# One decoder block on one core: weights stored in tiles, and two other ways to feed the gate and up products

## The chip, the cores and the metric

The kernel runs on 1 core of one Trainium2 chip. The time is device microseconds of one execution. Beside the timed runs there is one profiled execution, from which every duration below is taken. TensorE multiplies, VectorE (DVE in the profile) and ScalarE (ACT) work on tiles, SyncE (SP) issues the transfers, and PSUM is where TensorE's products land, in banks of 512 float32 columns.

## The reference

One decoder layer for 256 tokens of width 2048, all in float32:

```
h    = rmsnorm(x)
proj = h @ w_in                      # 2048 x 13328, for three branches and their gates
three branches (gated linear attention, stick-breaking attention,
cross-attention into 256 memory tokens), each projected to 2048
x    = x + (sum of sigmoid(gate) * branch) @ w_o
h2   = rmsnorm(x)
gate, up = split(h2 @ w_gate_up)     # 2048 x (5632 + 5632)
x    = x + (silu(gate) * up) @ w_down # 5632 x 2048
```

The change touches all large products by the layout of their weights, and the gate and up products of the last two lines by more than that.

## The kernel before, in words

**The large product.** Each large product goes through one function, `gemm`. It makes a block of 256 tokens x 512 columns as two PSUM tiles of 128 tokens (tag `acc`, four of them, so two blocks). To keep float32 accuracy, both sides are split into a high and a low part of few significant bits (`split`), in a type that TensorE multiplies in one pass (F32R), and three products are added: high times high, high times low, low times high. The activations (128 x 128 pieces of `hh` and `hl`, in other stages `xTh`/`xTl`, `oh`/`ol`, `fh`/`fl`) are the stationary operand, loaded by one LDWEIGHTS for each product (PEld in the profile); the weights (`whi`, `wlo`, 512 columns) are the moving operand, which is streamed past it.

**The staging.** A transfer on SyncE's queue brings 4 chunks of 128 weight rows x 512 columns (1 MB) into a tile `raw` (three buffers). The chunks are split in pairs: ScalarE copies a pair to `whi` (CAST, 128 x 1024), VectorE subtracts it from `raw` to give `wlo` (TENSOR_TENSOR, 128 x 1024). There are four buffers of each. A pair then feeds 12 products: for each of the two token tiles, for each of its two chunks, the three terms, on lines 169, 170 and 171.

**The order of the work.** The engines run their own instruction streams in the order in which a scheduler has put them; it goes by the order of the code and by when it expects operands and buffers. After each pair `step()` lets some small background work in, such as the transposes of a block of results (`to_chunks`, TensorE line 177).

**The feed-forward part.** For each of 11 blocks of 512 hidden columns: `gemm` for the gate (16 chunks, that is 8 pairs, 96 products), SiLU on ScalarE into `f_s` (line 717, two instructions), `gemm` for up (the same size), VectorE multiplies it into `f_s` (line 720), and `to_chunks` transposes and splits the block into `fh`/`fl` during the gate products that follow. After blocks 0 to 5 and 6 to 10 the down projection runs over what is there.

The lines of `before` that the prediction needs are 118 and 119 (the split), 158 (the load), 169 to 171 (the products), 177 (transposes), 475 to 477 (a small product for the low-rank columns with 256 moving columns), 357 (attention scores of plain float32), 717 and 720.

Of the kernel before, what the change touches and what calls it, by code (L numbers as in the profile page):

```python
# [10 lines left out]
F32R = mybir.dt.float32r  # L11
# [5 lines left out]
P = 128  # L17
# [12 lines left out]

O_GQ, O_GK, O_GV, O_GR, O_GA = 0, 512, 1024, 2048, 3072
O_SQ = O_GA + GR
O_SK, O_SV, O_MQ, O_G = O_SQ + MIX, O_SQ + 2 * MIX, O_SQ + 3 * MIX, O_SQ + 4 * MIX

# the gains, as columns of 128 rows
VECS = {
# [8 lines left out]
}  # L45
# constants that depend on shapes alone: for float32 operands, then for one-pass products
C_ID, C_STRICT, C_CAUSAL = 0, P, 2 * P
# [24 lines left out]
def trunk(ctx: ExitStack, tc: tile.TileContext, a, out):  # L72
# [18 lines left out]

    # ---- work that runs beside the large products: generators, advanced a step at a time
    background = []
# [12 lines left out]
    def pipelined(stages, n, gap):  # L106
        """One item enters per round; each of its stages comes gap rounds after the one before."""
        for r in range(n + gap * (len(stages) - 1)):
            for i in reversed(range(len(stages))):
                j = r - gap * i  # L110
                if 0 <= j < n:
                    stages[i](j)
                    yield

    def split(hi, lo, src, scale=None):
        """hi + lo = src (* scale), each part of 12 significant bits or fewer."""
        if scale is None:
            act.copy(hi, src)  # L118
            dve.tensor_tensor(lo, src, hi.bitcast(F32), op=ALU.subtract)  # L119
        else:  # L120
            act.activation(hi, src, AF.Copy, scale=scale)
            dve.scalar_tensor_tensor(lo, src, scale, hi.bitcast(F32), op0=ALU.mult, op1=ALU.subtract)

    def rsqrt_mean(ss, n, width):
        """(ss / n + eps) ** -0.5 of a [P, width] tile."""
        m = small.tile([P, width], F32, name="rs_m", bufs=4)
# [17 lines left out]

    def gemm(xs, w, c0, row0=0, first=()):
        """[T, NB] = xs.T @ w[row0*128.., c0:c0+NB] as two PSUM tiles of 128 tokens.
        xs: per chunk of 128 rows the high and low parts [P, T], or what loads them.
        first: the numbers of chunks in the first loads, where not KG."""
        o = [acc() for _ in range(2)]
        nk = len(xs)  # L150
        sizes = list(first)
        sizes += [min(KG, nk - k) for k in range(sum(sizes), nk, KG)]
        k0 = 0
        for n in sizes:
            xp = [x() if callable(x) else x for x in xs[k0 : k0 + n]]
            raw = loads()
            r0 = (row0 + k0) * P
            nc.sync.dma_start(raw[:, :n], w[r0 : r0 + n * P, c0 : c0 + NB].rearrange("(g p) n -> p g n", p=P))
            for g in range(0, n, 2):
                m = min(2, n - g)  # L160
                wh = wp.tile([P, 2, NB], F32R, tag="whi", name="whi")
                wl = wp.tile([P, 2, NB], F32R, tag="wlo", name="wlo")
                split(wh[:, :m], wl[:, :m], raw[:, g : g + m])
                for t in range(2):
                    s = slice(t * P, (t + 1) * P)
                    for j in range(m):
                        xh, xl = xp[g + j]
                        k = k0 + g + j
                        pe.matmul(o[t][:], xh[:, s], wh[:, j], start=k == 0, stop=False)  # L169
                        pe.matmul(o[t][:], xh[:, s], wl[:, j], start=False, stop=False)  # L170
                        pe.matmul(o[t][:], xl[:, s], wh[:, j], start=False, stop=k == nk - 1)  # L171
                step()
            k0 += n
        return o
# [4 lines left out]
    def load_T(pool_, name, src, gain, stage):  # L179
        """The transposed activations [D, T] times the gain, split, as chunks; the loads are traced  # L180
        where a chunk is first asked for."""
        hi = pool_.tile([P, KD, T], F32R, name=f"{name}h", tag=f"{name}h", bufs=1)
# [15 lines left out]
    def token_rstd(name, src, r, n):  # L198
        """(mean of squares of each row + eps) ** -0.5 into r [P, 2], its negative into n."""
        ss = const.tile([P, 2], F32, name=f"{name}_ss")  # L200
        for t in range(2):
            x = loads()[:].rearrange("p g n -> p (g n)")
            nc.sync.dma_start(x, src[t * P : (t + 1) * P, :])
            act.activation(x, x, AF.Square, accum_out=ss[:, t : t + 1])
            yield
        y = rsqrt_mean(ss[:], D, 2)
        dve.tensor_copy(r[:], y)
        dve.tensor_scalar(n[:], y, -1.0, None, op0=ALU.mult)

# [46 lines left out]

    # ---- the memory's keys and values
    w_in, w_kv = a["w_in"], a["w_mem_kv"]
# [44 lines left out]
    later, ones, tri, rest = (cr[:, i : i + P] for i in (R_LATER, R_ONES, R_TRI, R_REST))  # L303
    # q of the stick-breaking heads takes the factor d ** -0.5 with its gain
    g_sqs = const.tile([P, 1], F32, name="g_sqs")
# [40 lines left out]

    # ---- cross-attention into the memory
    o_mem = outT()
# [62 lines left out]

    # ---- stick-breaking attention
    o_sb = outT()
    W = 3 * P

    def diagonal(x):
        """Columns [0, 128) and [256, 384): the blocks on the diagonal."""
        return x[:, :W].rearrange("p (b q) -> p b q", b=3)[:, 0:3:2, :]
# [41 lines left out]

    # the low-rank columns as the stationary operand (with their neighbours): transposed at once
    a2 = att.tile([GR, 512], F32, name="a2", bufs=1)
# [3 lines left out]
    raw = wp.tile([P, KD, P], F32, tag="raw", name="raw_a", bufs=3)  # L466
    nc.sync.dma_start(raw[:], w_in[:, O_GA : O_GA + P].rearrange("(k p) n -> p k n", p=P))
    p = tmp()
# [13 lines left out]
    def sigmoid(dst, o, t, table):  # L482
        """Of the rows of o times their rstd; without the table, with the functions that the
        attentions hold loaded: exp(-log(1 + exp(-v)))."""
        if table:
# [9 lines left out]

    # ---- gated linear attention
    S = [att.tile([P, GDV], F32, name=f"S{h}", bufs=1) for h in range(GH)]
# [4 lines left out]
    def gla():  # L502
        for t in range(2):
# [57 lines left out]
            for c in range(2):  # L561
                s = slice(c * GC, (c + 1) * GC)
                for h in range(GH):
                    if c == 0:
                        # the first start clears what the bank has accumulated, for both of its heads
                        pe.matmul(ov[h], sT[:, h], vh[h], start=h % 2 == 0, stop=False, skip_group_check=True)  # L566
# [68 lines left out]

    # ---- merge of the branches
    merged = main.tile([P, 2, D], F32, name="merged", tag="resid")
# [19 lines left out]
    def turned_merged(n):  # L657
        i = n // NB
        if i % 2 == 0:
            # blocks 0 and 1 take the place of the stick-breaking heads', 2 and 3 that of the gates' inputs  # L660
            tm.append(
# [16 lines left out]

    # ---- output projection and residual
    hh = xpool.tile([P, KD, T], F32R, name="hh", tag="xTh")  # L680
# [22 lines left out]

    # ---- SwiGLU, the down projection in two parts of the hidden width
    ffn = ctx.enter_context(tc.tile_pool(name="ffn", bufs=1))
# [5 lines left out]
    for part in (range(0, 6), range(6, NF)):  # L711
        fs = []
        for j in part:
            g = gemm(hs, a["w_gate_up"], j * NB)
            sg = ffn.tile([P, 2, NB], F32, name="f_s", bufs=2)
            for t in range(2):
                act.activation(sg[:, t], g[t][:], AF.Silu, scale=r2[:, t : t + 1])
            u = gemm(hs, a["w_gate_up"], FF + j * NB)
            for t in range(2):
# [4 lines left out]
        for n in range(0, D, NB):  # L724
            o = gemm(fs, a["w_down"], n, row0=4 * part[0])
            for t in range(2):
                # the last piece in halves, so that its stores begin sooner
                half = NB // 2 if part[-1] == NF - 1 and n + NB == D else NB
# [37 lines left out]
```

## Time and profile before

| | |
|---|---|
| time, median of 2 runs | 1744.97 us (1744.42 to 1745.52) |
| span of the profiled execution | 1740.1 us |
| time less span | 4.9 us |
| TensorE busy, matrix products | 1728.5 us, 99%, 7588 records |
| TensorE busy, weight loads | 1387.5 us, 80% |
| VectorE busy | 924.7 us, 53% |
| ScalarE busy | 783.1 us, 45% |
| transfers | 321.8 MB, mean 185 GB/s |
| granted TensorE clock | 1.000 |

The profiled execution's own time is its span and the 4.9 us around it; its spans and the timed runs are compared on that footing. Rows of the time order have, from left to right, the start and the duration in us, the engine, the line of the kernel, the operation, output<-inputs, shapes, and how many records were merged. A product's duration of 0.39 to 0.40 us is modelled and overlaps the next one; what counts is the distance from one start to the next. In rows of groups the two numbers behind the bar are the busy time in us and the mean duration in ns, then the idle time before and what ended it.

### The profile page before, as it was taken

The numbers are of one execution on the slowest core, as the hardware profiler recorded it, in microseconds if no ns is written. First come the engines' busy times: TensorE is split into PE (matmuls) and PEld (weight loads), VectorE is DVE, ScalarE is ACT, GpSimd is POOL, SyncE is SP. The second block draws the span as 40 slices with busy tenths as digits, with TensorE's granted clock in tenths as the row PEclk, the third lists the DMA queues.
The fourth block names the chain that finished last, engine by engine and source line by source line (L and its number), as shares of the span: only waits on it lengthen the run. The fifth ranks groups of instructions, "written<-read, shape, count | busy, mean of one in ns | idle before, by whom it ended". The sixth has DMA issues, their size and how long they took to land.

```text
span 1740.1 us, 18823 instructions
## 1 busy us (share of the span) xinstructions
PE 1728.5 (99%) x7588; PEld 1387.5 (80%) x7588; DVE 924.7 (53%) x1082; ACT 783.1 (45%) x932; POOL 1.3 (0%) x6
## 2 busy tenths in 40 slices
PE   8999999999999999999999999999999999999999
PEld 6888888888777888888888888888888888888887
DVE  5756565664565555545555644444444444444543
ACT  6654444654554454344444444444433334444332
POOL 0000000000000000000000000000000000000000
PEclk9999999999999999999999999999999999999999
DMA  8775445445444565555556555555555555555553
GB/s 306 261 237 181 145 156 183 153 159 183 159 145 141 186 206 186 188 182 193 176 187 198 189 184 179 193 179 184 191 173 192 194 187 177 192 178 185 190 208 110
DMA packets 164310, 321.81 MB, mean 185 GB/s; under 512 B 5488, under 2 KB 12144, under 8 KB 163712
## 3 DMA queue, kind: packets, MB, share of 16 engines
q1 hardware_dynamic: 164048, 320.33, 54.7%
q8 instruction: 59, 0.97, 0.2%
q10 hardware_dynamic: 176, 0.30, 0.1%
q14 instruction: 27, 0.22, 0.0%
HBM read 318.50 MB, written 2.10 MB: 184 GB/s over the span
## 4 chain that ended last, share of the span: by engine, by line
PE 99%; DMA 1%; DVE 0%; ACT 0%; SPq 0%; issue 0%; DVEq 0%
PE acc L169 31%; PE acc L170 31%; PE acc L171 31%; PE tmp L177 2%; DMA raw<-in_w_mem_kv 1%; PE tmp L385 0%; PE tmp L357 0%; PE tmp L573 0%; PE tmp L568 0%; PE tmp L566 0%; PE tmp L442 0%; PE tmp L451 0%; PE tmp L425 0%; PE tmp L505 0%; PE tmp L475 0%; PE tmp L476 0%
## 5 line engine op out<-in xcount | busy, mean ns | idle before, releaser
L119 DVE TENSOR_TENSOR wlo<-raw,whi 128x1024 fp32r<-128x1024 f32 (+1 forms) x585 | 715.1, 1223 | 729.4 <-ACT whi L118 729.0
L118 ACT CAST whi<-raw 128x1024 fp32r<-128x1024 f32 (+1 forms) x585 | 611.4, 1046 | 870.2 <-PE acc L171 847.6
L169 PE MATMUL acc<-whi,xTh 128*128 128x512 f32 x832 | 335.4, 403 | 0.0
L171 PE MATMUL acc<-whi,xTl 128*128 128x512 f32 x832 | 329.1, 395 | 0.0
L170 PE MATMUL acc<-wlo,xTh 128*128 128x512 f32 x832 | 329.0, 395 | 0.0
L169 PE MATMUL acc<-whi,hh 128*128 128x512 f32 x704 | 279.9, 398 | 0.0
L171 PE MATMUL acc<-whi,hl 128*128 128x512 f32 x704 | 278.2, 395 | 0.0
L170 PE MATMUL acc<-wlo,hh 128*128 128x512 f32 x704 | 278.1, 395 | 0.0
L171 PEld LDWEIGHTS acc<-whi,xTl 128*128 128x128 f32 x832 | 156.0, 188 | 38.2 <-issue 0.3
L169 PEld LDWEIGHTS acc<-whi,xTh 128*128 128x128 f32 x832 | 156.2, 188 | 36.3 <-ACT whi L118 0.8
L170 PEld LDWEIGHTS acc<-wlo,xTh 128*128 128x128 f32 x832 | 156.3, 188 | 35.5 <-issue 0.7
L171 PEld LDWEIGHTS acc<-whi,hl 128*128 128x128 f32 x704 | 132.0, 188 | 32.2
L170 PEld LDWEIGHTS acc<-wlo,hh 128*128 128x128 f32 x704 | 132.1, 188 | 31.3
L169 PEld LDWEIGHTS acc<-whi,hh 128*128 128x128 f32 x704 | 132.1, 188 | 31.3
L169 PE MATMUL acc<-whi,fh 128*128 128x512 f32 x352 | 139.4, 396 | 0.0
L171 PE MATMUL acc<-whi,fl 128*128 128x512 f32 x352 | 139.1, 395 | 0.0
L170 PE MATMUL acc<-wlo,fh 128*128 128x512 f32 x352 | 139.1, 395 | 0.0
L169 PE MATMUL acc<-whi,oh 128*128 128x512 f32 x256 | 102.2, 399 | 0.0
L171 PE MATMUL acc<-whi,ol 128*128 128x512 f32 x256 | 101.3, 396 | 0.0
L170 PE MATMUL acc<-wlo,oh 128*128 128x512 f32 x256 | 101.2, 395 | 0.0
L171 PEld LDWEIGHTS acc<-whi,fl 128*128 128x128 f32 x352 | 66.0, 188 | 16.1
L169 PEld LDWEIGHTS acc<-whi,fh 128*128 128x128 f32 x352 | 66.0, 188 | 16.0
(205 smaller groups left out, 1191.1 us busy)
## 6 DMA issues: line engine op xcount, KB each, us to landing
raw<-in_w_in SPq DMA_DIRECT2D x104, 1024.0 KB, 5.0
raw<-in_w_gate_up SPq DMA_DIRECT2D x88, 1024.0 KB, 5.0
raw<-in_w_down SPq DMA_DIRECT2D x44, 1024.0 KB, 5.0
raw<-in_w_o SPq DMA_DIRECT2D x16, 1024.0 KB, 5.1
raw<-in_w_mem_kv SPq DMA_DIRECT2D x15, 1024.0 KB, 6.1
raw<-in_w_br_mem SPq DMA_DIRECT2D x8, 1024.0 KB, 5.0
raw<-in_w_br_sb SPq DMA_DIRECT2D x8, 1024.0 KB, 5.0
raw<-in_w_br_gla SPq DMA_DIRECT2D x8, 1024.0 KB, 5.0
```

Of the source, the lines that this page charges most:

```text
L118: act.copy(hi, src)
L119: dve.tensor_tensor(lo, src, hi.bitcast(F32), op=ALU.subtract)
L169: pe.matmul(o[t][:], xh[:, s], wh[:, j], start=k == 0, stop=False)
L170: pe.matmul(o[t][:], xh[:, s], wl[:, j], start=False, stop=False)
L171: pe.matmul(o[t][:], xl[:, s], wh[:, j], start=False, stop=k == nk - 1)
L177: pe.transpose(dst, src, ident)
```

## The change

It does three things.

1. **Tiled weights.** All large weights are laid out anew in memory before the launch, as [column block of 512][row within the chunk, 128][chunk][512 columns]. A load then reads, for each of the 128 partitions, one stretch of 4 x 2 KB where it read four stretches of 2 KB before. The 16 low-rank columns of `w_in` and their 112 neighbours become an array of their own (`w_ga`), read as 8 KB per partition, and the other columns of `w_in` move up by 16.
2. **Gate products, form "turns".** The 12 products of a pair change order: chunk, then term, then token tile. Each two neighbours have the same moving operand and write to the two PSUM tiles in turn.
3. **Up products, form "mixed".** High and low part of a pair share one tile `both` of 128 x 2 chunks x 512 columns x 2 parts; column n's high and low part lie next to each other. The CAST, the subtraction and the moving operand thus step over every other element (8 bytes from one to the next). `both` has two buffers, where `whi` and `wlo` have four each.

All other products keep the old form ("bank"). The core of the diff (removed comments left out):

```diff
-    def gemm(xs, w, c0, row0=0, first=()):
+    def gemm(xs, w, c0, row0=0, first=(), form="bank"):
...
-            r0 = (row0 + k0) * P
-            nc.sync.dma_start(raw[:, :n], w[r0 : r0 + n * P, c0 : c0 + NB].rearrange("(g p) n -> p g n", p=P))
+            r0 = row0 + k0
+            nc.sync.dma_start(raw[:, :n], w[c0 // NB, :, r0 : r0 + n])
             for g in range(0, n, 2):
                 m = min(2, n - g)
-                wh = wp.tile([P, 2, NB], F32R, tag="whi", name="whi")
-                wl = wp.tile([P, 2, NB], F32R, tag="wlo", name="wlo")
+                if form == "mixed":
+                    both = ffn.tile([P, 2, NB, 2], F32R, tag="both", name="both", bufs=2)
+                    wh, wl = both[:, :, :, 0], both[:, :, :, 1]
+                else:
+                    wh = wp.tile([P, 2, NB], F32R, tag="whi", name="whi")
+                    wl = wp.tile([P, 2, NB], F32R, tag="wlo", name="wlo")
                 split(wh[:, :m], wl[:, :m], raw[:, g : g + m])
-                for t in range(2):
-                    s = slice(t * P, (t + 1) * P)
-                    for j in range(m):
-                        xh, xl = xp[g + j]
-                        k = k0 + g + j
-                        pe.matmul(o[t][:], xh[:, s], wh[:, j], start=k == 0, stop=False)
-                        pe.matmul(o[t][:], xh[:, s], wl[:, j], start=False, stop=False)
-                        pe.matmul(o[t][:], xl[:, s], wh[:, j], start=False, stop=k == nk - 1)
+                def product(t, j, i):
+                    xh, xl = (x[:, t * P : (t + 1) * P] for x in xp[g + j])
+                    k = k0 + g + j
+                    pe.matmul(o[t][:], (xh, xh, xl)[i], (wh, wl, wh)[i][:, j],
+                              start=k == 0 and i == 0, stop=k == nk - 1 and i == 2)
+                if form == "turns":
+                    order = [(t, j, i) for j in range(m) for i in range(3) for t in range(2)]
+                else:
+                    order = [(t, j, i) for t in range(2) for j in range(m) for i in range(3)]
+                for q in order:
+                    product(*q)
...
-            g = gemm(hs, a["w_gate_up"], j * NB)
+            g = gemm(hs, a["w_gate_up"], j * NB, form="turns")
...
-            u = gemm(hs, a["w_gate_up"], FF + j * NB)
+            u = gemm(hs, a["w_gate_up"], FF + j * NB, form="mixed")
...
+    def tiled(w):
+        k, n = w.shape
+        return np.ascontiguousarray(w.reshape(k // P, P, n // NB, NB).transpose(2, 1, 0, 3))
```

**Where instructions move.** In the rows below, numbers tell buffers apart, and the shape is that of the output. First TensorE in the middle of a gate block; `acc` with the even and the odd number are the block's two token tiles. Before:

```order
L169 MATMUL acc_8035<-whi_8039,hh_6457 128x512
L170 MATMUL acc_8035<-wlo_8040,hh_6457 128x512
L171 MATMUL acc_8035<-whi_8039,hl_6458 128x512
L169 MATMUL acc_8035<-whi_8039,hh_6457 128x512
L170 MATMUL acc_8035<-wlo_8040,hh_6457 128x512
L171 MATMUL acc_8035<-whi_8039,hl_6458 128x512
L169 MATMUL acc_8036<-whi_8039,hh_6457 128x512
```

After the change, the same place in the pair `whi_7842`:

```order
L176 MATMUL acc_7722<-whi_7842,hh_6457 128x512
L176 MATMUL acc_7723<-whi_7842,hh_6457 128x512
L176 MATMUL acc_7722<-wlo_7843,hh_6457 128x512
L176 MATMUL acc_7723<-wlo_7843,hh_6457 128x512
L176 MATMUL acc_7722<-whi_7842,hl_6458 128x512
L176 MATMUL acc_7723<-whi_7842,hl_6458 128x512
```

Six products in a row went to one PSUM tile; now each goes to the other one than its predecessor. The number of products is the same.

Second, TensorE where an up block ends and the next gate block begins. Before, the last pair of up (`whi_8015`, into `acc_7894`) is followed by the first of the gate (`whi_8039`, into `acc_8035`):

```order
L169 MATMUL acc_7894<-whi_8015,hh_6457 128x512
L170 MATMUL acc_7894<-wlo_8016,hh_6457 128x512
L171 MATMUL acc_7894<-whi_8015,hl_6458 128x512
L169 MATMUL acc_8035<-whi_8039,hh_6457 128x512
L170 MATMUL acc_8035<-wlo_8040,hh_6457 128x512
```

After the change, at the last but one pair of up (`both_7977`, into `acc_7877` and `acc_7878`):

```order
L176 MATMUL acc_7878<-both_7960,hl_6458 128x512
L176 MATMUL acc_7877<-both_7977,hh_6457 128x512
L176 MATMUL acc_7878<-both_7977,hh_6457 128x512
L176 MATMUL acc_8011<-whi_8015,hh_6457 128x512
L176 MATMUL acc_8012<-whi_8015,hh_6457 128x512
L176 MATMUL acc_8011<-wlo_8016,hh_6457 128x512
L176 MATMUL acc_7877<-both_7977,hh_6457 128x512
L176 MATMUL acc_7877<-both_7977,hl_6458 128x512
```

Three products of the coming gate block (`acc_8011`, `acc_8012`) now stand between the high part of that pair and its low part.

Third, ScalarE from the SiLU of one block on. Before:

```order
L717 ACTIVATE f_s_7890<-acc_7739,r2_7107 128x512
L118 CAST whi_7947<-raw_7929 128x1024
L118 CAST whi_7965<-raw_7963 128x1024
L118 CAST whi_7981<-raw_7963 128x1024
L118 CAST whi_7999<-raw_7997 128x1024
L118 CAST whi_8015<-raw_7997 128x1024
L118 CAST whi_8039<-raw_8037 128x1024
```

After the change:

```order
L735 ACTIVATE f_s_7874<-acc_7723,r2_7107 128x512
L119 CAST both_7913<-raw_7911 128x1024
L119 CAST both_7928<-raw_7911 128x1024
L119 CAST both_7945<-raw_7943 128x1024
L119 CAST both_7960<-raw_7943 128x1024
L119 CAST whi_8015<-raw_8013 128x1024
L119 CAST whi_8038<-raw_8013 128x1024
L119 CAST both_7977<-raw_7975 128x1024
L119 CAST both_7992<-raw_7975 128x1024
```

The first two copies of the next gate block (`whi_8015`, `whi_8038`) now stand ahead of the last two of up (`both_7977`, `both_7992`); VectorE's subtractions follow the same order.

More of the change, by code (lines that the diff above doesn't have):

```diff
@@ L29 @@
 TAU = 16.0
-O_GQ, O_GK, O_GV, O_GR, O_GA = 0, 512, 1024, 2048, 3072
-O_SQ = O_GA + GR
+A_GA = 3072
+O_GQ, O_GK, O_GV, O_GR, O_SQ = 0, 512, 1024, 2048, 3072
 O_SK, O_SV, O_MQ, O_G = O_SQ + MIX, O_SQ + 2 * MIX, O_SQ + 3 * MIX, O_SQ + 4 * MIX
@@ L156, in gemm @@
             raw = loads()
-            r0 = (row0 + k0) * P
-            nc.sync.dma_start(raw[:, :n], w[r0 : r0 + n * P, c0 : c0 + NB].rearrange("(g p) n -> p g n", p=P))
+            r0 = row0 + k0
+            nc.sync.dma_start(raw[:, :n], w[c0 // NB, :, r0 : r0 + n])
             for g in range(0, n, 2):
                 m = min(2, n - g)
-                wh = wp.tile([P, 2, NB], F32R, tag="whi", name="whi")
-                wl = wp.tile([P, 2, NB], F32R, tag="wlo", name="wlo")
-                split(wh[:, :m], wl[:, :m], raw[:, g : g + m])
-                for t in range(2):
-                    s = slice(t * P, (t + 1) * P)
-                    for j in range(m):
-                        xh, xl = xp[g + j]
-                        k = k0 + g + j
-                        pe.matmul(o[t][:], xh[:, s], wh[:, j], start=k == 0, stop=False)
-                        pe.matmul(o[t][:], xh[:, s], wl[:, j], start=False, stop=False)
-                        pe.matmul(o[t][:], xl[:, s], wh[:, j], start=False, stop=k == nk - 1)
+                if form == "mixed":
[4 more added lines that the diff above has]
+                    wl = wp.tile([P, 2, NB], F32R, tag="wlo", name="wlo")
+                split(wh[:, :m], wl[:, :m], raw[:, g : g + m])
+                def product(t, j, i):
+                    xh, xl = (x[:, t * P : (t + 1) * P] for x in xp[g + j])
+                    k = k0 + g + j
+                    pe.matmul(
+                        o[t][:],
+                        (xh, xh, xl)[i],
+                        (wh, wl, wh)[i][:, j],
+                        start=k == 0 and i == 0,
+                        stop=k == nk - 1 and i == 2,
+                    )
+                if form == "turns":
[4 more added lines that the diff above has]
+                    product(*q)
                 step()
@@ L466, in trunk @@
     raw = wp.tile([P, KD, P], F32, tag="raw", name="raw_a", bufs=3)
-    nc.sync.dma_start(raw[:], w_in[:, O_GA : O_GA + P].rearrange("(k p) n -> p k n", p=P))
+    nc.sync.dma_start(raw[:], a["w_ga"])
     p = tmp()
@@ L751 @@
     }
+    def tiled(w):
+        k, n = w.shape
+        return np.ascontiguousarray(w.reshape(k // P, P, n // NB, NB).transpose(2, 1, 0, 3))
+    w = v["w_in"]
+    arrays["w_in"] = tiled(np.concatenate([w[:, :A_GA], w[:, A_GA + GR :]], 1))
+    arrays["w_ga"] = np.ascontiguousarray(w[:, A_GA : A_GA + P].reshape(KD, P, P).transpose(1, 0, 2))
+    arrays["gla_w_a2"] = v["gla_w_a2"]
     arrays["vecs"] = np.concatenate([cols(v[n]) for n in VECS], 1)
-    for n in ("w_in", "w_mem_kv", "gla_w_a2", "w_br_gla", "w_br_sb", "w_br_mem", "w_o", "w_gate_up", "w_down"):
-        arrays[n] = v[n]
+    for n in ("w_mem_kv", "w_br_gla", "w_br_sb", "w_br_mem", "w_o", "w_gate_up", "w_down"):
+        arrays[n] = tiled(v[n])
     nc = bacc.Bacc("TRN2", target_bir_lowering=False, num_devices=1)
```

## The prediction

> **What bounds the kernel now.** I read the page's engines and its chain of waits first, then the windows, then the time order of TensorE.
>
> ```profile
> span 1740.1 us, 18823 instructions
> PE 1728.5 (99%) x7588; PEld 1387.5 (80%) x7588; DVE 924.7 (53%) x1082; ACT 783.1 (45%) x932; POOL 1.3 (0%) x6
> PE 99%; DMA 1%; DVE 0%; ACT 0%; SPq 0%; issue 0%; DVEq 0%
> ```
>
> TensorE is busy for all but 11.6 us and the chain is TensorE for 99%. A busy TensorE says little, since the products' ends are modelled; so the question is at what distance they start.
>
> ```profile
> 0.00:20.00 20.00, 12.18 (x41) 8.80 (x42) 9.96 (x18) 11.15 (x19) 0.20 (x4) 1.00 0.84 281
> 1000.00:1700.00 700.00, 700.00 (x3049) 563.60 (x3048) 337.74 (x303) 283.73 (x292) 0.00 (x0) 1.00 0.56 186
> 1099.72 0.39 PE L169 MATMUL acc<-whi,hh 128*128 128x512 f32 x1
> 1099.96 0.40 PE L170 MATMUL acc<-wlo,hh 128*128 128x512 f32 x1
> ...
> 1105.79 0.39 PE L171 MATMUL acc<-whi,hl 128*128 128x512 f32 x1
> ```
>
> The feed-forward stage (1000 to 1700 us) has no idle TensorE at all. From 1099.72 to 1105.79 stand 27 products: 6.07 us over 26 gaps, 0.2335 us each, all 0.23 or 0.24. Only two things can move the time: this distance, or a stall put in its place. Idle time to be won back lies nearly all in the first 20 us (7.8 of 11.6 us).
>
> What sets 0.2335 us? Three more rows tell. The first two are products of the same kind before the clock is up; the next two are one-pass products with 256 moving columns, 18 in a row; the last is eight records of plain float32 products with 256 columns.
>
> ```profile
> 8.23 0.63 PE L169 MATMUL acc<-whi,mTh 128*128 128x512 f32 x1
> 10.36 0.51 PE L171 MATMUL acc<-whi,mTl 128*128 128x512 f32 x1
> 407.17 0.28 PE L475 MATMUL tmp<-xTh,whi_a 128*128 128x256 f32 x1
> 409.18 0.28 PE L477 MATMUL tmp<-xTh,wlo_a 128*128 128x256 f32 x1
> 176.63 1.73 PE tmp L357 x8
> ```
>
> - Slow clock: 2.13 us over five gaps, 0.426 us, or 0.83 ns a column.
> - Plain float32: 1.73/8 = 0.216 us for 256 columns, 0.84 ns a column.
> - One pass at the full clock: 2.01/17 = 0.1182 us for 256 columns, 0.2335 us for 512. The difference gives 0.4504 ns a column and leaves 2.9 ns a product.
>
> So the one-pass stream, the only one that takes a new 4-byte column at the full rate, runs at 0.450 ns where half of the slow rate would be 0.416: it loses 8% column by column, and hardly anything per product. A loss that appears only at the highest reading rate looks like an operand that just fails to arrive in time. That is my reading, not a row.
>
> **The change part by part.**
>
> *Gate products in turn.* The number, shape and operands of the products stay; 1056 of them change order. What an alternation of PSUM tiles or a repeated operand could save is a cost per product: at most the 2.9 ns, 1056 x 2.9 ns = 3 us. The 27 rows above hold a change of PSUM tile after every sixth product and show neither a longer nor a shorter gap there. Bounds: -3 to +3 us; I take 0. Token tile 0 now ends one product before tile 1 instead of six, so the first SiLU starts some 1.2 us later; ScalarE's next copy waits longer than that anyway (below).
>
> *Up products, two parts side by side.* This is the large term.
>
> ```profile
> L169 PE MATMUL acc<-whi,hh 128*128 128x512 f32 x704 | 279.9, 398 | 0.0
> L170 PE MATMUL acc<-wlo,hh 128*128 128x512 f32 x704 | 278.1, 395 | 0.0
> L171 PE MATMUL acc<-whi,hl 128*128 128x512 f32 x704 | 278.2, 395 | 0.0
> ```
>
> These are 2112 products of gate and up, so 1056 of up. Each still has 512 moving columns, but they are spread over 4096 bytes of each partition instead of 2048. No row of this trace has a moving operand with gaps, so the cost is bounded: below by 0.213 us (half of the slow clock's 0.426: the 8% loss gone), 1056 x -0.0205 = -22 us; in the middle by the contiguous 0.2335, zero; above by a column that takes twice as long, 512 x 0.9008 ns + 2.9 ns = 0.464 us, 1056 x 0.2306 = +243.5 us. Between lies 0.426 us, the distance at half the clock: 1056 x 0.1925 = +203 us. I take the upper end: the stream is, by the 8%, already short of what it asks for with every byte passed over in use; with every other byte in use, the same supply brings half the columns.
>
> The Trainium skill speaks against that: "Advanced Engine Details and Errata", section SBUF Cachelines, says that on-chip memory is read in lines of 16 bytes and that two hits on a line suffice to hide its access; steps of 8 bytes give just two. By that rule the term is zero. The skill's "TensorE: Matmul & The Clock Gate" gives 215.7 ns from start to start for a bf16 product of 512 columns; 233 ns here agrees with a supply already at its limit when the operand is twice as wide, which the rule does not foresee.
>
> *Splitting into the shared tile.* The count of instructions stays (16 CASTs and 16 subtractions per block of gate and up). Their writing steps over 8 bytes, and `both` has two buffers, not four.
>
> ```profile
> L118 ACT CAST whi<-raw 128x1024 fp32r<-128x1024 f32 x583 | 610.1, 1048 | 867.8 <-PE acc L171 847.6 <-DMA raw<-in_w_mem_kv 6.9 <-PE tmp L476 2.9
> L119 DVE TENSOR_TENSOR wlo<-raw,whi 128x1024 fp32r<-128x1024 f32 x583 | 713.7, 1225 | 726.9 <-ACT whi L118 726.5
> 1034.76 0.39 PE L171 MATMUL acc<-whi,hl 128*128 128x512 f32 x1
> 1035.19 1.05 ACT L118 CAST whi<-raw 128x1024 fp32r<-128x1024 f32 x1 [1.75 <-PE acc L171]
> 1104.12 1.05 ACT L118 CAST whi<-raw 128x1024 fp32r<-128x1024 f32 x1 [1.18 <-PE acc L171]
> 1105.21 1.23 DVE L119 TENSOR_TENSOR wlo<-raw,whi 128x1024 fp32r<-128x1024 f32 x1 [1.00 <-ACT whi L118]
> ```
>
> The pair's last product starts at 1034.76, and the copy into its buffer 0.43 later, 0.20 after the pair's time is up. Then 1.05 of copy, 0.04 to the subtraction, 1.23: refilled 2.52 us after release. With two buffers TensorE has one pair left, 12 x 0.2335 = 2.80 us, and needs the low part 0.23 later still: 0.5 us to spare at today's distance, 3 us at 0.464. One place is tighter: two copies of the next gate block stand ahead of the seventh pair (the third piece of order above). Counted from the start of up, the sixth pair's copy ends at 12.45, those two at 14.55, the seventh's at 15.60; VectorE comes to 13.71, 16.17, 17.40. TensorE starts that pair at 16.80, but its low part stands behind five high-part and gate products, at 17.97. Cover 0.5 us; a late load could eat it. So 0 to 1 us for all 11 blocks at today's distance, 0 at 0.464. If the stepping itself made copy and subtraction slower, 0.5 us is all that hides it (a rival below). Queued behind the waiting copies are the transposed block's copies (`fh`), needed a whole block later.
>
> *Tiled weights.*
>
> ```profile
> raw<-in_w_gate_up SPq DMA_DIRECT2D x88, 1024.0 KB, 5.0
> 6.48 0.80 PE L169 MATMUL acc<-whi,mTh 128*128 128x512 f32 x1 [6.48 <-ACT whi L118]
> 8.00 6.12 DMA raw<-in_w_mem_kv
> ```
>
> A load lands 5.0 us after issue, a block of two pairs lasts 5.6 us, and three buffers hold: loads are hidden behind products everywhere but at the start, and a longer landing would be too. At the start, 6.48 us pass to the first product; its load is one chunk, whose pieces of 2 KB stay as long as they were. The other 1.34 us of idle time (20 - 12.18 - 6.48) hang on loads like the one at 8.00. Bounds -1.3 to +1; I take -1. SyncE's list of loads keeps its order; the low-rank load changes its pieces and had no TensorE idle at it.
>
> *Sum.* 1740.1 + 243.5 - 1 = 1982.6 us of span, + 4.9 around it = **1987 us**. Span plus 4.9 is the median of the runs, 1744.97, by the way the 4.9 is formed.
>
> **Rivals.**
>
> *The gaps cost nothing (0.2335 us stays).* For it: ScalarE, VectorE and TensorE have covers of 0.5 us, and the loss of 8% need not come from memory. Against: that loss. It gives 1745 - 1 + 0 to 1, **1745 us**; it decides if the moving operand is fetched at least twice as fast as it is used. This is also the skill's rule of two hits, and the case in which the kernel is not slower.
>
> *A part of the gaps shows.* If the 8% are a short stop at every so many bytes passed over, twice the bytes bring twice the stops: 512 x (0.416 + 2 x 0.034) ns + 2.9 ns = 0.251 us, + 0.0175 x 1056 = 18 us, **1762 us**. For it: it explains the 8% without a hard limit. Against: nothing shows single stops.
>
> *Copies and subtractions slow down.* If writing over 8 bytes took double, the refill would be 0.20 + 2.10 + 0.04 + 2.46 = 4.80 us; the low part would be due 0.23 after the pair's start, so a pair lasts 4.57 instead of 2.80 us: 88 x 1.77 = +156, **1900 us**. Nothing speaks for it but that no row has such a write; it does nothing if the products take 0.464 us, since a pair then lasts 5.57 us.
>
> *The reading gets better.* If the 8% were lost in the shared PSUM tile or the dense operand, gate or up could fall to 0.213 us: -22 us each, **1700 to 1723 us**. The unchanged gap at changes of tile speaks against the first; nothing shown speaks for the second.
>
> **How the numbers follow.** Chances: twice the column time 0.56 (own range 1947 to 1995: 0.426 to a little over 0.467 us); no cost 0.24; partial 0.12; slow copies 0.03; better 0.05. Within 2% (35 us, about what a measurement of this kernel can tell from no change) lie no cost, three quarters of partial and a part of better: 0.24 + 0.09 + 0.02 = 0.35. Slower by more: 0.56 + 0.03 + 0.03 = 0.62. Faster by more: 0.03. To hold 8 in 10, the range must reach from the likeliest to the no-cost case: 1743 to 1998 us; about 0.85 lies in it, the ends being rivals, not noise.
>
> **What the profile after would show.** Up products (`acc<-both`) at 0.46 us from start to start, gate and down at 0.2335: the main step is right. At 0.2335 it is wrong; at 0.25 the partial rival holds. Gate products below 0.230 would refute that alternation is worth nothing. ScalarE's CAST into `both` over 1.1 us, or VectorE's over 1.3, with TensorE idle before `both` rows, is the slow-copy rival. TensorE idle in the first 20 us between 6.3 and 7.8 us is the tiling's small term. The prediction is wrong above all if memory can deliver more than the one-pass stream takes, and the 8% have another cause.

## The result, and the profile after

The changed kernel takes **1974.19 us** (median of 2 runs, 1974.16 to 1974.22) against 1744.97 us: a ratio of 1.1318, with a 95% interval of 1.1294 to 1.1343. The forecast was 1987 us.

The head of the page of the changed kernel: the span, the busy time of each engine, and the shares of the chain of waits that ended last.

```profile
span 1972.4 us, 18755 instructions
PE 1961.3 (99%) x7588; PEld 1408.3 (71%) x7588; DVE 921.0 (47%) x1082; ACT 782.4 (40%) x932; POOL 1.3 (0%) x6
PE 99%; DMA 1%; DVE 0%; ACT 0%; SPq 0%; issue 0%; DVEq 0%
```

The span is longer by 1972.4 - 1740.1 = 232.3 us, and TensorE's busy time by 232.8. The number of matrix products is the same, 7588. So TensorE doesn't wait more (11.1 us idle in the whole span, where it was 11.6), it takes longer. The windows (window and length, then busy time and records of PE, PEld, DVE, ACT and POOL, granted clock, DMA share, GB/s) say the same of the feed-forward stage:

```profile
0.00:20.00 20.00, 12.70 (x40) 8.72 (x41) 10.09 (x19) 11.73 (x20) 0.20 (x4) 1.00 0.79 277
1000.00:1700.00 700.00, 700.00 (x2268) 435.43 (x2267) 242.95 (x220) 207.72 (x214) 0.00 (x0) 1.00 0.37 137
```

Again no idle TensorE from 1000 to 1700 us and the full clock, but 2268 records where there were 3049. The time order of TensorE shows which ones take longer, at the place where three products of the next gate block's first pair stand between those of up:

```profile
1038.01 0.63 PE L176 MATMUL acc<-both,hl 128*128 128x512 f32 x1
1038.46 1.09 PE L176 MATMUL acc<-both,hh 128*128 128x512 f32 x2
1039.37 0.63 PE L176 MATMUL acc<-both,hl 128*128 128x512 f32 x1
...
1042.55 1.08 PE L176 MATMUL acc<-both,hh 128*128 128x512 f32 x2
1043.45 0.64 PE L176 MATMUL acc<-whi,hh 128*128 128x512 f32 x2
1043.92 0.39 PE L176 MATMUL acc<-wlo,hh 128*128 128x512 f32 x1
1044.15 0.61 PE L176 MATMUL acc<-both,hh 128*128 128x512 f32 x1
```

Products that read `both` follow each other at 1.36/3 = 0.453 us (1038.01 to 1039.37). The three that read `whi` and `wlo`, 1043.45 to 1044.15, take 0.70/3 = 0.233. The step from one distance to the other comes with the operand, from one product to the next. Over all 1056 products of up the mean distance is 0.4528 us, and that of gate and down is still 0.2335. The extra is 1056 x (0.4528 - 0.2335) = **231.6 us**, and the spans differ by 232.3.

Groups by form (busy us, mean ns of one, then idle time before and what ended it) for the two engines that fill `both`:

```profile
L119 ACT CAST both<-raw 128x1024 fp32r<-128x1024 f32 x88 | 97.9, 1115 | 266.4 <-PE acc L176 265.9 <-DMA raw<-in_w_gate_up 0.5
L120 DVE TENSOR_TENSOR both<-raw,both 128x1024 fp32r<-128x1024 f32 x88 | 107.7, 1224 | 377.4 <-ACT both L119 377.4
L176 PE MATMUL acc<-both,hh 128*128 128x512 f32 x704 | 383.6, 631 | 0.0
```

Writing over 8 bytes makes the copy 6% longer (1115 against 1048 ns) and the subtraction no longer (1224 against 1225). The 0.0 behind the bar of TensorE's row is its idle time before these products: none of it waits for `both`.

### The profile page after: what moved, and what is told of

It is laid out like the page before. It is cut to its first block, busy times and chain, and to the rows that moved or that the text cites. A ratio compares the mean times of both kernels' runs of the same rounds, so it can differ in the third digit from the quotient of the medians.

```text
span 1972.4 us, 18755 instructions
## 1 busy us (share of the span) xinstructions
PE 1961.3 (99%) x7588; PEld 1408.3 (71%) x7588; DVE 921.0 (47%) x1082; ACT 782.4 (40%) x932; POOL 1.3 (0%) x6
## 4 chain that ended last, share of the span: by engine, by line
PE 99%; DMA 1%; DVE 0%; ACT 0%; SPq 0%; issue 0%; DVEq 0%
PE acc L176 95%; PE tmp L195 1%; DMA raw<-in_w_mem_kv 1%; PE tmp L403 0%; PE tmp L375 0%; PE tmp L591 0%; PE tmp L586 0%; PE tmp L584 0%; PE tmp L460 0%; PE tmp L469 0%; PE tmp L443 0%; PE tmp L523 0%; PE tmp L493 0%; PE tmp L494 0%; PE tmp L495 0%; PE tmp L568 0%
## 5 line engine op out<-in xcount | busy, mean ns | idle before, releaser
L120 DVE TENSOR_TENSOR wlo<-raw,whi 128x1024 fp32r<-128x1024 f32 (+1 forms) x497 | 604.7, 1221 | 518.6 <-ACT whi L119 518.0
L119 ACT CAST whi<-raw 128x1024 fp32r<-128x1024 f32 (+1 forms) x497 | 517.3, 1046 | 731.3 <-PE acc L176 710.2
L176 PE MATMUL acc<-both,hh 128*128 128x512 f32 x704 | 383.6, 631 | 0.0
L120 DVE TENSOR_TENSOR both<-raw,both 128x1024 fp32r<-128x1024 f32 x88 | 107.7, 1224 | 377.4 <-ACT both L119 377.4
L176 PEld LDWEIGHTS acc<-both,hh 128*128 128x128 f32 x704 | 145.3, 206 | 166.5 <-issue 165.0
L176 PE MATMUL acc<-both,hl 128*128 128x512 f32 x352 | 222.3, 632 | 0.0
L119 ACT CAST both<-raw 128x1024 fp32r<-128x1024 f32 x88 | 97.9, 1115 | 266.4 <-PE acc L176 265.9
L176 PE MATMUL acc<-whi,hh 128*128 128x512 f32 x352 | 112.3, 400 | 0.0
L176 PE MATMUL acc<-wlo,hh 128*128 128x512 f32 x352 | 112.1, 395 | 0.0
L176 PE MATMUL acc<-whi,hl 128*128 128x512 f32 x352 | 110.6, 395 | 0.0
```

Source lines behind the costliest of these rows:

```text
L176: pe.matmul(o[t][:], (xh, xh, xl)[i], (wh, wl, wh)[i][:, j], start=k == 0 and i == 0, stop=k == nk - 1 and i == 2,)
```

## The experiments

The first three take the change apart. The kernel before ran at 1742.32 us (median of 21 runs) beside these three, at 1744.21 (1 run) beside the next four and at 1742.55 (7 runs) beside the last five. The runs from the fourth experiment on were timed once each, except the one with two-byte parts in all large products (4 runs); what they show rests on the distances of hundreds of products in each trace, not on the totals. All edits are against the changed kernel, except where another is named.

### The tiling alone

```diff
-            g = gemm(hs, a["w_gate_up"], j * NB, form="turns")
+            g = gemm(hs, a["w_gate_up"], j * NB, form="bank")
...
-            u = gemm(hs, a["w_gate_up"], FF + j * NB, form="mixed")
+            u = gemm(hs, a["w_gate_up"], FF + j * NB, form="bank")
```

> Tiled weights alone; gate and up products in the old form. Theory (loads are hidden behind products but for the start): 1744 us, 0 to 1.5 us below before, TensorE idle in the first 20 us 7.3 us. Rival (the shorter list of pieces frees TensorE of something in the middle): more than 3 us below before, products closer than 0.2335 us.

Measured: 1743.43 us, ratio 1.0001 (0.9992 to 1.001); products 0.2335 us apart, span 1740.2. The window of the first 20 us:

```profile
0.00:20.00 20.00, 13.55 (x42) 9.26 (x43) 10.06 (x18) 11.45 (x19) 0.20 (x4) 1.00 0.80 284
```

TensorE is busy for 13.55 us of it where it was 12.18 before and is 12.70 in the changed kernel. That is no clear gain of the layout, since single profiles differ by as much. With the new layout the next run has 12.58 us there, and the third, on the old layout, 12.77. The total shows nothing either: the new layout is worth nothing that 11 runs can tell.

### The turns

```diff
-            u = gemm(hs, a["w_gate_up"], FF + j * NB, form="mixed")
+            u = gemm(hs, a["w_gate_up"], FF + j * NB, form="bank")
```

> Tiled weights and gate products in turn, up products in the old form. Theory (no cost or gain per product in alternating): as e1 within 3 us, 1744 us, gate products at 0.2335 us from start to start. Rival (alternating PSUM tiles or repeating the moving operand saves a part of the 8%): gate products at 0.216 us, 18 us below e1.

Measured: 1743.21 us, ratio 1.0 (0.9991 to 1.0009). The time order of gate products, which now come in pairs with the same operand:

```profile
1099.87 0.63 PE L176 MATMUL acc<-whi,hh 128*128 128x512 f32 x2
1100.34 0.63 PE L176 MATMUL acc<-wlo,hh 128*128 128x512 f32 x2
1100.81 0.63 PE L176 MATMUL acc<-whi,hl 128*128 128x512 f32 x2
1101.27 0.63 PE L176 MATMUL acc<-whi,hh 128*128 128x512 f32 x2
```

1.40 us for six products: 0.233. Neither the repeated operand nor the turn of PSUM tiles shortens anything.

### Side by side alone

The edit is on the kernel before: old layout, old order of the gate, only up in the shared tile.

```diff
+                if form == "mixed":
+                    both = ffn.tile([P, 2, NB, 2], F32R, tag="both", name="both", bufs=2)
+                    wh, wl = both[:, :, :, 0], both[:, :, :, 1]
```

> The up products with high and low parts side by side, alone, on the weights and the gate products of before. Theory (the whole loss is the reading of the moving operand with gaps): up products at 0.4528 us, 1056 x 0.2193 = 232 us more than before, 1977 us. Rival (the three parts of the change act together): less than 1950 us or up products at another distance.

Measured: 1974.93 us, ratio 1.1332 (1.1311 to 1.1352), span 1972.6. The whole loss is this one part. What is left to find out is why an operand with gaps takes 0.453 us.

### What in the gaps costs: runs of two columns, and a step of 16 bytes

Gate gets runs of two high columns, then two low ones (`runs`); up gets the parts of both chunks of a pair side by side, so that a column follows the last one at 16 bytes (`step`).

```diff
+                if form == "step4":
+                    both = ffn.tile([P, NB, 4], F32R, tag=form, name=form, bufs=2)
+                    both = both[:].rearrange("p n (j h) -> p j n h", h=2)
...
+                elif form.startswith("runs"):
+                    run, off = int(form[4]), int(form[6])
+                    both = ffn.tile([P, 2, 2 * NB + 8], F32R, tag=form, name=form, bufs=2)
+                    both = both[:, :, off : off + 2 * NB].rearrange("p j (n h c) -> p j n h c", h=2, c=run)
```

> Tiled weights. Gate: two columns of the high part (8 bytes, starting on a multiple of 8), then two of the low part. Up: the parts of two chunks side by side, so that a column is 16 bytes from the next. Three theories. Pieces of 8 bytes (each reading brings an aligned pair of columns, and the stream takes one reading per pair at its best): gate 0.2335 us, up 0.453 us, sum 1745 + 232 = 1977 us. Lines of 16 bytes: gate 0.453, up 0.9 us, 1745 + 232 + 704 = 2680 us. The step alone (any step other than 1 halves the rate, whatever memory holds): gate 0.2335, up 0.453, 1977 us.

Measured: 2218.53 us, span 2216.8. TensorE in time order, first gate, then up; then ScalarE's copy into the tile with 16 bytes of step:

```profile
1001.50 0.63 PE L192 MATMUL acc<-runs,hl 128*128 128x512 f32 x1
1001.95 1.09 PE L192 MATMUL acc<-runs,hh 128*128 128x512 f32 x2
1002.86 0.65 PE L192 MATMUL acc<-runs,hl 128*128 128x512 f32 x1
...
1039.68 0.64 PE L192 MATMUL acc<-step,hl 128*128 128x512 f32 x1
1040.14 1.10 PE L192 MATMUL acc<-step,hh 128*128 128x512 f32 x2
1041.06 0.64 PE L192 MATMUL acc<-step,hl 128*128 128x512 f32 x1
L119 ACT CAST step<-raw 128x1024 fp32r<-128x1024 f32 x88 | 181.9, 2093 | 213.0 <-PE acc L192 213.0
```

From start to start runs of two take 1.36/3 = 0.453 us and the step of 16 bytes 1.38/3 = 0.460 (medians over all such products: 0.453 and 0.462). None of the three theories gave both: the runs aren't fast, so it is not pieces of 8 bytes; the wider step hardly adds, so it is not each 16-byte stretch at its price; and the runs have no constant step, so it is not the step as such. The copy, which had grown by 6% at 8 bytes, takes double at 16 (2093 ns).

### Runs that start 4 bytes later, and one column read 512 times

```diff
-            g = gemm(hs, a["w_gate_up"], j * NB, form="turns")
+            g = gemm(hs, a["w_gate_up"], j * NB, form="runs2_1")
...
+                    return cut(x) if form != "step0" else x[:, 0:1].to_broadcast([P, NB])
```

> Tiled weights. Gate: runs of two columns as in the run before, but the tile begins 4 bytes later, so that each run straddles a multiple of 8. Up: each product reads column 0 of its part 512 times instead of 512 columns, which changes what the up products compute and leaves their number and size. Pieces of 8 bytes: gate 0.453 us (+232 us). The step alone: gate 0.2335. If the 8% by which contiguous reading falls short are the memory's, up falls to 0.216 us or less (-18 us); if they belong to the one-pass product itself, up stays at 0.2335. Sums: 8 bytes and memory 1958 us, 8 bytes and product 1977 us, step and memory 1726 us, step and product 1744 us.

Measured: 1960.69 us. Runs of two: 0.453 us (median), at this start as at the other. One column read over and over; the second row is 18 products behind the first:

```profile
1049.67 0.38 PE L192 MATMUL acc<-whi,hh 128*128 128x512 f32 x1
...
1053.56 0.38 PE L192 MATMUL acc<-whi,hh 128*128 128x512 f32 x1
```

3.89/18 = 0.216 us from start to start, where 512 different neighbours take 0.2335. So TensorE itself takes a 4-byte column in 0.216/512 us = 0.42 ns, and the 8% above that, on which the prediction had built, is the time to bring different columns.

### Runs of four

Gate in runs of four columns that begin at a multiple of 16 bytes (`runs4_0`), up in the same runs 4 bytes later (`runs4_1`).

> Tiled weights. Gate: runs of four columns (16 bytes, starting on a multiple of 16). Up: the same runs, starting 4 bytes later. Pieces of 8 bytes: gate 0.2335, up three pieces instead of two per run, 0.343 us (+116 us), 1860 us. Lines of 16 bytes: gate 0.2335, up two lines instead of one per run, 0.453 us, 1977 us. The step alone: both 0.2335, 1744 us.

Measured: 1978.63 us, where the reading by 16-byte stretches had given 1977. Up first, then gate (both have the name `runs`):

```profile
1016.26 1.11 PE L192 MATMUL acc<-runs,hh 128*128 128x512 f32 x2
1017.17 0.66 PE L192 MATMUL acc<-runs,hl 128*128 128x512 f32 x1
1017.63 1.11 PE L192 MATMUL acc<-runs,hh 128*128 128x512 f32 x2
...
1058.64 0.62 PE L192 MATMUL acc<-runs,hh 128*128 128x512 f32 x2
1059.10 0.39 PE L192 MATMUL acc<-runs,hl 128*128 128x512 f32 x1
1059.33 0.63 PE L192 MATMUL acc<-runs,hh 128*128 128x512 f32 x2
```

Up takes 1.37/3 = 0.457 us, gate 0.69/3 = 0.230 (medians over all of them: 0.455 and 0.232). The two differ by nothing but where the runs begin. Half of the bytes passed over lie idle in both, so idle bytes aren't the cost. What separates these forms is the number of aligned stretches of 16 bytes: 512 columns in whole stretches touch 128 of them; runs of four that begin 4 bytes later touch 256, as do runs of two and a step of 8 bytes, and these three take 0.453 to 0.457 us. The step of 16 bytes, with 512 stretches at 0.462 us, doesn't fit; it stays open below.

### Parts of two bytes

The parts of gate and up, weights and activations, become bf16: contiguous in gate, side by side in up, where a column is now 4 bytes from the last one.

```diff
-                    both = ffn.tile([P, 2, NB, 2], F32R, tag="both", name="both", bufs=2)
+                    both = ffn.tile([P, 2, NB, 2], BF16, tag="both", name="both", bufs=2)
...
-    hh = xpool.tile([P, KD, T], F32R, name="hh", tag="xTh")
+    hh = xpool.tile([P, KD, T], BF16, name="hh", tag="xTh")
```

> Tiled weights; activations and weights of gate and up split into bf16 parts (coarser rounding than before), so that a column is 2 bytes. Gate: contiguous. Up: high and low side by side, a column 4 bytes from the next. If the 8% come from the width of the operand, gate products stand at 0.216 us (-18 us). Pieces of 8 bytes: up passes over as many bytes as a contiguous float32 operand, 0.2335 us or less, sum about 1726 us. The step alone: up at 0.43 us, sum 1745 - 18 + 207 = 1934 us.

Measured: 1718.47 us, span 1716.7.

```profile
L182 PE MATMUL acc<-both,hh 128*128 128x512 bf16 x694 | 215.5, 387 | 2.5 <-DVE both L121 0.2
L182 PE MATMUL acc<-whi,hh 128*128 128x512 bf16 x352 | 133.4, 379 | 0.2
L120 ACT CAST both<-raw 128x1024 bf16<-128x1024 f32 x88 | 118.1, 1345 | 77.2 <-DVE both L121 41.0 <-PE acc L182 29.2 <-DMA raw<-in_w_gate_up 6.8
```

From start to start gate takes 0.216 us (64 stretches) and up 0.226 (128 stretches). So the same tile of high and low columns that doubles the time with 4 bytes costs 5% with 2, and a step as such isn't the cost.

### All large products with two-byte parts, in the old order

All operands of the large products are split into bf16 parts, which hold fewer bits than before; layout tiled, all forms "bank".

> Tiled weights, all large products in the old form, and both operands of all of them split into bf16 parts (8 significant bits each, so coarser rounding than before). Theory (a 2-byte operand arrives in time, 0.216 us): 7008 products x 0.0175 = 123 us less than before, 1621 us. Rival (the splits or the loads become the bound when a pair lasts 2.59 us instead of 2.80): over 1650 us, with TensorE idle between products.

Measured: **1621.24 us** (median of 4 runs), ratio **0.9299** (0.9284 to 0.9315), faster than both kernels. The page:

```profile
span 1620.3 us, 18823 instructions
PE 1605.1 (99%) x7588; PEld 764.2 (47%) x7588; DVE 923.7 (57%) x1082; ACT 780.4 (48%) x932; POOL 1.3 (0%) x6
L182 PE MATMUL acc<-whi,hh 128*128 128x512 bf16 x704 | 266.8, 379 | 0.0
```

The large products stand 0.216 us apart (median), and weight loads fall from 1387.5 to 764.2 us. The 8% is won where both operands are half as wide; that the streamed one is what counts was shown by the one column above, which left the loaded operand as it was.

### A late start without gaps, and a step of 32 bytes

Gate: contiguous columns that begin 4 bytes late. Up: 32 bytes from column to column, in a tile that has room for one buffer only, so TensorE has to wait for its refills.

```diff
+                if form == "off1":
+                    wh = ffn.tile([P, 2, NB + 8], F32R, tag="oh1", name="oh1", bufs=2)[:, :, 1 : NB + 1]
...
+                elif form == "step8":
+                    both = ffn.tile([P, NB, 8], F32R, tag=form, name=form, bufs=1)
```

> Tiled weights. Gate: contiguous weights, but the tile begins 4 bytes after a multiple of 16. Up: a column is 32 bytes from the next. Theory A (columns are taken four at a time from the first on; a four that lies in one line of 16 bytes comes at the full rate, one that touches two or more comes at half): gate 0.453 us, +232 us; up 0.462, +241 us; 2218 us. Theory B (what counts is how many columns each line gives in all; the start adds one line to 128): gate 0.2335; up 0.462; 1986 us. In both, a wider step than 16 bytes costs no more than 16; if each line had its own price, up would be above 0.9 us.

Measured: 2187.95 us, with a mean granted clock of 0.934. The total can't be compared with either theory's, because of the waits for the single buffer:

```profile
L199 PE MATMUL acc<-step,hh 128*128 128x512 f32 x704 | 397.3, 634 | 170.2 <-ACT step L119 117.0 <-DVE step L120 53.1
```

The distances can. Gate in time order, seven products from the first row to the last:

```profile
999.80 0.40 PE L199 MATMUL acc<-oh,hh 128*128 128x512 f32 x1
...
1001.22 0.41 PE L199 MATMUL acc<-oh,hh 128*128 128x512 f32 x1
```

That is 1.42/6 = 0.237 us, and 0.236 in the median of all, where theory A had 0.453: 129 stretches instead of 128, and a late start as such, cost next to nothing. Up takes 0.431 us, a little less than at 16 bytes, at a granted clock of 1.0 (441 of 588 distances) as at 0.5 (362 of 468); most of the others hold a wait.

### Two-byte parts with steps of 8 and 16 bytes

> As the run with bf16 parts in gate and up, but gate with a column 8 bytes from the next, up with 16 bytes. Theory A (four at a time, one line or more): gate 0.453 us, up 0.462 us, 1745 + 232 + 241 = 2218 us. Rival (a 2-byte operand has twice the allowance in bytes, as the step of 4 bytes at 0.226 us could also be read): gate 0.23 us, up 0.45, 1975 us.

Measured: 2758.2 us; neither theory had that. Gate takes 0.4515 us (256 stretches), as theory A had it, but up 0.900 (512 stretches). The second number has two possible causes: the stretches, or the clock, which was lowered at just that time, after stalls of some 4 us where up begins:

```profile
1000.00:1026.00 26.00, 26.00 (x59) 6.68 (x57) 12.45 (x6) 17.12 (x6) 0.00 (x0) 0.99 0.31 112
1048.00:1106.00 58.00, 58.00 (x66) 8.12 (x65) 28.53 (x7) 28.68 (x7) 0.00 (x0) 0.50 0.15 54
```

The first window holds gate products, the second up products. Whether the gaps make 0.900 us or the clock does is not to be told from these rows; the next run was made for that.

### A step of 16 bytes beside contiguous two-byte columns

The edit is against the run before.

```diff
-                    gaps = 4 if c0 < FF else 8
-                    both = ffn.tile([P, NB, gaps], BF16, tag=f"step{gaps}", name=f"step{gaps}", bufs=2)
+                    gaps = 8
+                    both = ffn.tile([P, NB, gaps], BF16, tag=f"step{gaps}", name=f"step{gaps}", bufs=3)
...
-            g = gemm(hs, a["w_gate_up"], j * NB, form="mixed")
+            g = gemm(hs, a["w_gate_up"], j * NB, form="half")
```

> The parts of gate and up are bf16 again. The gate products read contiguous columns (0.216 us each when alone), the up products step over 16 bytes, from a tile with three buffers, so that TensorE should not stall much where up begins. Disputed is what made the 0.900 us of such products in the run with both steps: the stretches of 16 bytes that a product touches, or the clock, which was granted at 0.5 there. By the stretches (128 of them took 0.226 us and 256 took 0.4515, so 1.76 ns each, and 512 take 0.90 us): up 0.900 us from its first product on, whatever clock is granted, and gate products that stand between up products keep 0.216 to 0.43 us; the span is that of the run with bf16 parts side by side, 1716.7, plus 1056 x (0.900 - 0.226) = 712, about 2428 us. By a floor of two cycles per column and a clock halved by stalls: without stalls the clock stays at 1.0 and up products take 0.45 to 0.46 us; 1716.7 + 1056 x 0.226 = 1955 us; where the clock is halved, 0.90 us appears only after a stall.

Measured: 2545.04 us, span 2543.3. First the start of an up block, then its end, in time order; then two windows between:

```profile
1017.32 0.38 PE L184 MATMUL acc<-wlo,hh 128*128 128x512 bf16 x1
1017.53 0.38 PE L184 MATMUL acc<-whi,hl 128*128 128x512 bf16 x1
1017.75 1.96 PE L184 MATMUL acc<-step,hh 128*128 128x512 bf16 x2
1019.53 1.08 PE L184 MATMUL acc<-step,hl 128*128 128x512 bf16 x1
...
1104.13 0.60 PE L184 MATMUL acc<-whi,hh 128*128 128x512 bf16 x1
1104.53 0.63 PE L184 MATMUL acc<-wlo,hh 128*128 128x512 bf16 x1
...
1107.87 0.38 PE L184 MATMUL acc<-whi,hh 128*128 128x512 bf16 x1
1108.08 0.38 PE L184 MATMUL acc<-wlo,hh 128*128 128x512 bf16 x1
1019.00:1022.00 3.00, 3.00 (x4) 0.35 (x3) 0.00 (x0) 0.00 (x0) 0.00 (x0) 1.00 0.00 0
1030.00:1100.00 70.00, 70.00 (x79) 9.83 (x78) 29.56 (x10) 26.26 (x9) 0.00 (x0) 0.50 0.20 75
```

Up takes 0.90 us from its first product on (1017.75 to 1019.53 holds two), right behind gate products at their full pace of 0.21. (The last gate pair had waited for its parts until 1010.05 and then run at half the clock, 0.43 us, until 1015.8; by 1017.75 that was over.) From 1019 to 1022 us the granted clock is 1.00, and all 68 distances of up that begin under a clock of 1.0 in this trace are 0.88 to 0.90 us. The clock falls after that: 0.50 in the second window, and the first gate products behind up still stand 0.43 apart, as at half the clock, until 1107.87. So the gaps make the 0.900 us, and the lowered clock comes with it: the theory of stretches holds here. The span is 115 us above that theory's 2428: 66 us are TensorE's idle time before `wlo` and `whi` products (57.6 + 8.6 us by the groups), and some 200 gate products at about 0.43 in place of 0.216 us make another 42 (an estimate).

### The stationary operand with gaps

The activations' parts lie side by side, so LDWEIGHTS steps over 8 bytes; gate and up are "bank". In some earlier stages the two parts of the activations share a tile, too, but each is still contiguous there.

```diff
-    hh = xpool.tile([P, KD, T], F32R, name="hh", tag="xTh")
-    hl = xpool.tile([P, KD, T], F32R, name="hl", tag="xTl")
+    hb = xpool.tile([P, KD, T, 2], F32R, name="hb", tag="xTh")
+    hh, hl = hb[:, :, :, 0], hb[:, :, :, 1]
```

> Tiled weights, weights contiguous in all products; in gate and up the activations' high and low part lie side by side, so the stationary operand is read with a column 8 bytes from the next. Theory (the load of the stationary operand runs beside the product before; even at twice its 188 ns it is partly hidden): if the load doubles to 0.376 us, products follow it at some 0.38 us, 2112 x 0.15 = +310 us, 2050 us. Rival (the stationary operand is read at a lower rate, so gaps cost it nothing): loads at 188 ns, 1744 us.

Measured: 1742.43 us, products 0.2335 us apart.

```profile
PE 1730.0 (99%) x7588; PEld 1406.9 (81%) x7588; DVE 924.9 (53%) x1082; ACT 782.9 (45%) x932; POOL 1.3 (0%) x6
L176 PEld LDWEIGHTS acc<-whi,hb 128*128 128x128 f32 x1408 | 277.1, 197 | 50.6
```

Weight loads take 1406.9 us in place of 1387.5: a load with gaps takes 197 ns where it took 188, not double, and all of it lies beside the products. Gaps of this size cost time in the operand that is streamed, not in the one that is loaded ahead. That needn't be another rule: a load of 128 columns at a step of 8 bytes touches 64 stretches, and at the 1.76 ns for a stretch that the two-byte runs gave, that is 113 ns (an estimate), less than the load takes anyway.

## Why the prediction was right, point by point

**The bound.** Right: TensorE never waited in the feed-forward stage, before or after, and only the distance of products could move the time. The reading of the 8% as an operand that just fails to arrive in time was only argued; the column read 512 times (0.216 us) shows it, and the two-byte parts (0.216) agree.

**Gate in turn: 0.** Right, 1.0 with 0.1% to either side. The gate's median distance is 0.234 us; single distances lie down to 0.226, as they did before the change (0.225).

**Up side by side: +243.5 us.** That the supply of the streamed operand is the limit was right, and the size 5% too high: 231.6 us. The mis-sized term is the distance, 0.464 forecast and 0.4528 measured. It came from doubling the whole column time of the contiguous operand (0.4504 ns), in place of the time that the stretches need. With two-byte parts 128 stretches take 0.226 us, and twice that is 0.452. By that, 0.0075 of the contiguous product's 0.2335 us would be something else, which doesn't double; that is argued from the two-byte runs, and not shown. The reason given, "with every other byte in use, the same supply brings half the columns", was right for this layout by luck: aligned runs of four pass over as many bytes and take 0.230. What doubles is the number of aligned 16-byte stretches touched, from 128 to 256.

**The rival of no cost (chance 0.24).** Wrong, and with it the rule of the Trainium skill in "Advanced Engine Details and Errata", section SBUF Cachelines, as the prediction read it: that section says that at least two hits on a 16-byte line are needed, and the prediction took two to be enough. Here two 4-byte columns per line take 0.453 us, and two 2-byte columns 0.4515. The line of 16 bytes agrees with the runs of four. Four hits of 4 bytes (0.2335) or of 2 bytes (0.226) were enough for TensorE's streamed operand; three in every line were not tried. The Trainium skill's figure of 215.7 ns in "TensorE: Matmul & The Clock Gate", section "Wait — 56ns, not 53.3ns?", which the prediction took for bf16, agrees with 0.216 here.

**The rivals of partial cost (0.251 us) and of better reading (0.213).** Wrong: no form with gaps had a usual distance between 0.24 and 0.43 us, and no 4-byte form that brings different columns one below 0.230.

**The split into the shared tile: no stall.** Right: 0.0 idle before `both` products. The copy grew by 67 ns to 1115, just past the 1.1 us named as a sign of the slow-copy rival; but the other half of that sign, TensorE idle before `both`, is missing, since a pair now lasts 12 x 0.453 = 5.4 us. The doubling that the rival had assumed comes at a step of 16 bytes (2093 ns), not at 8.

**Tiled weights: -1 us.** Not to be told from 0 (ratio 1.0001). TensorE's idle time in the first 20 us is 7.30 us in the changed kernel and 6.45 with the tiling alone, against 7.82. Both lie where the prediction had put them, but that is no clear sign of the tiling: side by side alone, on the old layout, has 7.23. The span with the tiling alone is 1740.2 us, as before.

**The sum.** 1987 forecast, 1974.2 measured. The 13 us are three errors: 11.9 us too much for up; 1.7 too little for the rest of the span (-1 forecast, 232.3 - 231.6 = +0.7 measured); and 3.1 too much around it. Time less span is 1974.2 - 1972.4 = 1.8 us here; for the kernel before it was 4.9 on the two runs that the forecast had, but 1742.3 - 1740.1 = 2.2 in a run beside the experiments, so it wasn't a fixed amount to add.

**What stays open.** With 2-byte columns the price follows the stretches all the way: 128, 256 and 512 take 0.226, 0.4515 and 0.900 us, 1.76 ns each. With 4-byte columns 128 and 256 do the same (0.2335 and 0.453), but 512 take only 0.462 at a step of 16 bytes and 0.431 at 32. Why 4-byte columns stop at about 0.45 us wasn't found. Nor was it found why the clock is lowered beside the 0.900 us stream, when it stays at 1.00 beside the 0.453 us stream of the changed kernel.

## What to carry to other kernels

When TensorE is busy all the time, measure the distance from start to start and hold it against the same product with a cheaper operand, such as one column read over and over. Here the product was 8% above that: the streamed operand came only just too late, and a layout that spread it over twice as many 16-byte stretches doubled the time. Interleave 4-byte parts in aligned runs of 16 bytes (0.230 us), not element by element (0.453), or put the gaps into the operand that is loaded ahead, where a step of 8 bytes cost no time. An operand half as wide won the 8% that three rearrangements could not touch, where its fewer bits are enough.

## What the runs showed of the hardware that was not expected

- The time of a streamed 4-byte operand jumps by a factor of two with a shift of its runs by 4 bytes (0.230 to 0.457 us), while a contiguous operand may start 4 bytes late for next to nothing (0.236 against 0.2335).
- Distances with wide gaps don't follow the granted clock: 0.431 us (4 bytes, step of 32) and 0.90 us (2 bytes, step of 16) at 1.0 as at 0.5, while contiguous two-byte columns go from 0.216 to 0.43.
- The granted clock fell to 0.5 beside a stream that never paused (70.00 us busy of 70.00) but took a column only every 1.76 ns; it fell some 4.7 us after that stream began (1017.75 to 1022.45 us).
- Copies and subtractions that write 4-byte elements over 8 bytes cost 1115 and 1224 ns, over 16 bytes 2093 and 2090; with 2-byte elements they took 1345 and 1315 ns over 4 bytes, and 4829 and 4888 over 16.
